# A hybrid conformer and attention layer on one core: first weights in common transfers, two statistics moved, the end reordered

## The chip, the core and the metric

The kernel runs on one core of a Trainium2 chip. The metric is the device time of one execution in microseconds; the number given for a kernel is the median of its runs. The core has TensorE (PE, matrix products into PSUM banks), VectorE (DVE), ScalarE (ACT), GpSimd (POOL) and SyncE (SP), which here only issues transfers (DMA). Each engine works through its own instructions in a fixed order, and waits for the others by semaphores. The order of an engine's instructions is set when the kernel is built; an instruction that waits holds up all that stand behind it on its engine.

## The reference

One layer on x (512 tokens x 2048), float32:

```python
xn = rms_norm(x, attn_norm_g[l])
proj = jnp.einsum("bsd,dc->bsc", xn, w_in[l])
u_val, u_gate, q, k, v = jnp.split(proj, split_pts, axis=-1)
y_conv = conformer_conv(u_val, u_gate, ...)      # GLU, depthwise conv 31, LayerNorm, silu
y_na = neighborhood_attention(heads(q), heads(k), heads(v), rpb[l])
mixed = concat([rms_norm(y_conv, conv_out_g[l]), rms_norm(y_na, na_out_g[l])])
x = x + jnp.einsum("bsc,cd->bsd", mixed, w_out[l])
xn = rms_norm(x, ffn_norm_g[l])
up = depthwise_conv(jnp.einsum("bsd,df->bsf", xn, w_up[l]), ffn_dw_w[l], ffn_dw_b[l])
gate, val = jnp.split(up, 2, axis=-1)
x = x + jnp.einsum("bsf,fd->bsd", silu(gate) * val, w_down[l])
return rms_norm(x, final_norm_g)
```

w_in is 2048 x 5120, w_out 2048 x 2048, w_up 2048 x 11264, w_down 5632 x 2048. In the text below "group A" is the convolution half, the first norm, the second norm and the final norm are the three rms_norm over 2048 columns.

## The kernel before, in words

**Arithmetic.** Each float32 operand of a product is split in two parts of the type fp32r, a high part (copied by ACT) and a low part (the rest, subtracted by DVE). A product is three matmuls: high x high, low x high, high x low (mm3, L124 to L129, so L127 to L129 stand for nearly all products). Weights come in units of 128 x 1024 (512 KB): SP loads them into one of 7 buffers "raw" (NR), ACT makes whi (L116), DVE makes wlo (L117), with four buffers each (NW = 4). `weights()` makes units up to three ahead (AHEAD) of the one that PE is at, along a list `plan`; so the whi of a unit is written into the buffer of the unit four earlier, and ACT's copy waits until PE has read that.

**Layout.** Activations lie as [128 columns, 512 tokens] tiles, 16 of them for 2048 columns. The norms' factors are per token, so they are applied after the products. `rsqrt_steps` (L179 to L212) makes such a factor: matmuls against a column of ones add up the squares over the partitions (L190), DVE and ACT take the inverse root (L192, and root in L172 to L177: Sqrt on ACT, four small DVE steps), DVE writes the result on the diagonals of two tiles dg (high L197, low L201, four instructions), and after `rest` yields two matmuls against a matrix of ones spread it over all partitions (L207); ACT copies it out of the bank (L211). Its bank is "po", one buffer, or "sc" with free=True.

**Order.** Statistics are generators. `tick(m)` (L134) stands behind groups of matmuls and takes the next step of the generator at the head of each of two lists, so the number of yields decides behind which product a step is put. `pin` keeps instructions in the order in which they are written; others are ordered by a scheduler's priorities when the kernel is built.

**The start (L214 to L255).** 16 tiles of x are loaded, and for each xh (ACT, times g1) and xl (DVE) are made. The first two output tiles (the gate's first and the value's first) are worked at once, k by k (`project_first`, L327), so that PE can follow the tiles of x as they arrive. Their weights, 2 x 2 units, come in ten transfers of 128 x 256 or 128 x 512 elements, between the tiles of x (`piece`, `pieces`). g1 comes by a DMA that ACT issues. Until the first data are there PE runs 20 matmuls on a tile "warm" that DVE makes (L233 to L240), whose results nobody reads.

**Group A (L372 to L401).** Runs beside the last projections and the attention: mean (L379), squares, the statistic "rln", normalisation and silu of eight tiles (the result, split, is `ma`), squares, the statistic "ra". The output projection starts with `out_half(ma, read_a)`: 16 output groups of 24 matmuls; `read_a` (L580) multiplies each by ra on DVE (oa, L585). There are three PSUM banks "mm" for these groups, so when ra is late the fourth group waits. The attention's last product ao also goes through the bank "po" (L495, copied by ACT in L507, squared in L510).

**Second norm and the MLP's up-projection.** `stats2` (L644) makes rstd2. The up-projection of a block f is a Strassen-like scheme of seven products (c = 0 to 6) of combined weights (`factors`, L655: c = 1, 4 and 6 need DVE additions into a tile ws, c = 2 into a raw) with combined inputs xc (L596 to L634). `up_apart` (L793) does it for f = 0 to 3 with 24 matmuls of 256 columns a product. For f = 0 the first three products run interleaved (L811). Banks: "mm" (three) for c = 0 to 5, "po" for c = 6 (L798). ACT copies the first two results (vv, L823), DVE adds the third; the fourth is copied in L826. `hidden` (L844) multiplies the two results by rstd2, does the depthwise convolution, silu and the product.

**The end (L910 to L998).** The last four f's part of the down-projection is computed last. For the first 384 tokens (fm) the output is kept transposed: 16 tiles, eight pairs, each multiplied by the final norm's factor (`finish`, L925) on DVE or, for some, by ACT and POOL (L932, L933), and sent out by SP (L937, L939), 3.1 MB in all. The last 128 tokens (tm) are computed token by token in four banks of 512 columns (L971 to L987), whose factor needs the sum of squares over all four banks (L981, L986 to L990); then four transfers of 256 KB (L998). `spread` puts the third statistic's L207 (by `next(stats)`), the copy rb (L966) and one pair at a time between the groups of these last matmuls.

## Time and profile before

| | |
|---|---|
| median of 3 runs | 2033.53 us (2030.55 to 2034.37) |
| profiled execution | 2030.16 us, its span 2028.4 us |
| granted clock, mean | 0.998 |
| ACT busy | 1050.9 us (52%) |
| DVE busy | 1675.5 us (83%) |
| bytes moved | 276.41 MB, 135 GB/s over the span |
| matmuls | 10672 |
| output tail: last matmul starts | 2018.94 us |

In rows of a timeline the first two numbers are the start and the busy time of one instruction, or of a run of equal ones (xN, then the busy time of all); then engine, line, operation, what is written <- what is read, shapes. The bracket at the end is the idle time of that engine just before and what ended it. Matmuls overlap in the records: the pace is read from start to start. "L127 MATMUL pu<-xc,whi" is the matmul of line 127 that writes a tile named pu. A row of windows has: the stretch, its length, busy time and number of instructions of PE, weight load, DVE, ACT and POOL, the granted clock, the share of the DMA engines, GB/s.

### The profile page before, as it was taken

The page shows a single profiled execution, that of the slowest core. Times are in us where ns is not written, and L with a number is a line of the kernel's source. Part 1 is how long each engine was busy: PE and PEld are TensorE (multiplying, and loading weights), DVE is VectorE, ACT ScalarE, POOL GpSimd, SP SyncE. Part 2 cuts the span into 40 slices and gives each one's busy share as a digit, 9 for nine tenths or more (in the row PEclk, how much of TensorE's full clock was granted, in tenths as well). Part 3 has the DMA queues.
Part 4 walks back from the last instruction along what each step waited for, and adds up shares of the span by engine and source line. Part 5 has one row for each costly group of instructions (what it writes and reads, how often), then busy time and mean ns, then how long its engine had stood idle before and what let it go on. Part 6 is the DMA issues. An engine that isn't in the chain of part 4 may idle for free.

```text
span 2028.4 us, 28313 instructions
## 1 busy us (share of the span) xinstructions
PE 2015.4 (99%) x10672; PEld 1726.5 (85%) x10672; DVE 1675.5 (83%) x2298; ACT 1050.9 (52%) x1674; POOL 159.5 (8%) x188
## 2 busy tenths in 40 slices
PE   9999999999999999999999999999999999999998
PEld 7888888888888998888888888888888888888887
DVE  7986888988577898888888888888888888889875
ACT  7323344466346555555555555555555555555563
POOL 0000000000001001111111111111111111110111
PEclk9999999999999999999999999999999999999999
DMA  7232333336347435566565565565565565564583
GB/s 256 83 104 84 114 94 109 109 124 215 108 120 178 120 114 146 123 147 146 125 146 146 128 142 146 128 142 146 121 149 146 125 146 146 127 144 127 144 206 126
DMA packets 97784, 276.41 MB, mean 136 GB/s; under 512 B 10992, under 2 KB 12784, under 8 KB 97648
## 3 DMA queue, kind: packets, MB, share of 16 engines
q1 hardware_dynamic: 72288, 228.45, 36.3%
q0 software_dynamic: 25216, 46.15, 15.5%
q8 instruction: 84, 1.38, 0.3%
q14 instruction: 52, 0.43, 0.1%
q10 hardware_dynamic: 144, 0.01, 0.0%
HBM read 220.04 MB, written 54.53 MB: 135 GB/s over the span
## 4 chain that ended last, share of the span: by engine, by line
PE 96%; DVE 2%; DMA 1%; ACT 0%; issue 0%; SPq 0%; ACTq 0%; DVEq 0%
PE pu L718 25%; PE pu L724 13%; PE pd L129 8%; PE pd L127 8%; PE pd L128 8%; PE pj L127 5%; PE pj L128 5%; PE pj L129 5%; PE po L127 3%; PE po L128 2%; PE po L129 2%; PE pv L313 1%; PE pv L312 1%; PE pv L314 1%; PE pu L127 1%; PE pu L129 1%
## 5 line engine op out<-in xcount | busy, mean ns | idle before, releaser
L116 ACT ACTIVATE whi<-raw 128x1024 fp32r<-128x1024 f32 x364 | 384.4, 1058 | 503.8 <-PE pj L128 136.6
L117 DVE TENSOR_TENSOR wlo<-raw,whi 128x1024 fp32r<-128x1024 f32 x364 | 444.4, 1221 | 214.0 <-ACT whi L116 205.2
L718 PE MATMUL pu<-xc,whi 128*128 128x512 f32 x2240 | 552.9, 391 | 0.0
L718 PEld LDWEIGHTS pu<-xc,whi 128*128 128x128 f32 x2240 | 413.0, 188 | 79.1
L724 PEld LDWEIGHTS pu<-xc,wlo 128*128 128x128 f32 x2240 | 292.3, 191 | 13.9
L724 PE MATMUL pu<-xc,wlo 128*128 128x256 f32 x2240 | 296.6, 283 | 0.0
L129 PE MATMUL pd<-hh,wlo 128*128 128x512 f32 x640 | 250.1, 391 | 0.0
L127 PE MATMUL pd<-hh,whi 128*128 128x512 f32 x640 | 249.6, 390 | 0.0
L128 PE MATMUL pd<-hl,whi 128*128 128x512 f32 x640 | 249.3, 390 | 0.0
L871 POOL DMA_DIRECT2D x2d<-pdc x160 | 139.4, 873 | 1162.4 <-ACT pdc L870 837.4
L128 PE MATMUL pj<-xl,whi 128*128 128x512 f32 x512 | 200.2, 391 | 0.1
L129 PE MATMUL pj<-xh,wlo 128*128 128x512 f32 x512 | 200.0, 391 | 0.0
L127 PE MATMUL pj<-xh,whi 128*128 128x512 f32 x512 | 198.9, 393 | 0.0
L750 ACT ACTIVATE pl<-pu 128x256 f32<-128x256 f32 x280 | 104.6, 382 | 143.5 <-PE pu L718 136.4
L116 ACT ACTIVATE whi<-ws 128x1024 fp32r<-128x1024 f32 x132 | 139.8, 1059 | 75.2 <-PE pu L718 58.2
L366 DVE SCALAR_TENSOR_TENSOR y<-ch,prm,y 128x500 f32<-128x500 f32 (+14 forms) x240 | 173.3, 740 | 4.3
L117 DVE TENSOR_TENSOR wlo<-ws,whi 128x1024 fp32r<-128x1024 f32 x132 | 161.1, 1220 | 13.9 <-ACT whi L116 13.6
L129 PEld LDWEIGHTS pd<-hh,wlo 128*128 128x128 f32 x640 | 120.1, 188 | 28.5 <-DVE wlo L117 3.3
L128 PEld LDWEIGHTS pd<-hl,whi 128*128 128x128 f32 x640 | 120.2, 188 | 24.9 <-DVE hl L856 0.3
L127 PEld LDWEIGHTS pd<-hh,whi 128*128 128x128 f32 x640 | 120.4, 188 | 22.6
L870 ACT ACTIVATE pdc<-pd 128x512 f32<-128x512 f32 x160 | 93.8, 588 | 79.3 <-PE pd L129 65.9
L127 PEld LDWEIGHTS pj<-xh,whi 128*128 128x128 f32 x512 | 96.3, 188 | 20.7 <-ACT xh L249 0.2
(204 smaller groups left out, 2886.4 us busy)
## 6 DMA issues: line engine op xcount, KB each, us to landing
raw<-in_w_up SPq DMA_DIRECT2D x176, 512.0 KB, 3.7
raw<-in_w_down SPq DMA_DIRECT2D x88, 512.0 KB, 4.0
x2d<-pdc POOLq DMA_DIRECT2D x160, 256.0 KB, 4.8
raw<-in_w_in SPq DMA_DIRECT2D x60, 512.0 KB, 3.8
raw<-in_w_out SPq DMA_DIRECT2D x32, 512.0 KB, 3.8
raw<-in_w_v SPq DMA_DIRECT2D x16, 512.0 KB, 4.1
tab<-in_tab SPq DMA_DIRECT2D x32, 256.0 KB, 5.0
x<-in_xG SPq DMA_DIRECT2D x16, 256.0 KB, 5.4
```

Source lines behind the costliest of these rows:

```text
L116: i = nc.scalar.activation(hi[:, :n], raw[:, :n], AF.Copy)
L117: j = nc.vector.tensor_sub(lo[:, :n], raw[:, :n], hi[:, :n].bitcast(F32))
L127: nc.tensor.matmul(ps, hi[:, a], mh, start=start, stop=False)
L128: nc.tensor.matmul(ps, hi[:, a], ml, start=False, stop=False)
L129: return nc.tensor.matmul(ps, lo[:, a], mh, start=False, stop=stop)
L312: nc.tensor.matmul(ps, xh, wh[:, f], start=kk == 0, stop=False)
L366: nc.vector.scalar_tensor_tensor(y[:, a:b], h[:, a + j - PAD:b + j - PAD], prm[:, o + j:o + j + 1], y[:, a:b], op0=ALU.mult, op1=ALU.add)
L718: i = nc.tensor.matmul(ps, w[0][:, k * P:(k + 1) * P], comb[c][k], start=k == 0, stop=stop and k == ks[-1])
L724: i = nc.tensor.matmul(ps[:, H:], w[1][:, k * P:(k + 1) * P], comb[c][k][:, :H], start=False, stop=stop and k == U - 1)
L750: nc.scalar.activation(to, ps, AF.Copy)
L870: nc.scalar.activation(t, ps, AF.Copy)
L871: nc.gpsimd.dma_start(xd[d], t, accum_op=ALU.add)
```

## The change

It has five parts.

1. **Start.** The host puts x0 and the 16 columns of g1 in one array x0 (128 x 528), loaded in one transfer into a "raw" buffer; ACT's DMA for g1 is gone, and g1 is copied to its tile by DVE. The weights of the two first output tiles are interleaved by k in one array w_a (128 x 4096), loaded in five pieces, k = 0; 1 to 3; 4 to 7; 8 to 11; 12 to 15, with rows of 1, 3, 4, 4 and 4 KB, issued behind x0, x1, x2, x6 and x10. For x0 the high part is made by DVE. The tile "warm" is a memset and the first thing on DVE; PE runs 7 idle matmuls.
2. **Group A.** One yield more ahead of "rln", one fewer ahead of "ra".
3. **First f.** Its product c = 3 uses the bank "po", and its c = 6 one of the banks "mm".
4. **Second norm.** rest = 4 instead of 2, so L207 comes two products later; the multiplication of the first f by rstd2 and all behind it (`gated_tile`) is issued in f = 1 behind c = 1 (`meanwhile`).
5. **End.** The four banks alternate between "sc" and "tr"; both L207 and rb come at (g, k) = (2, 2) of `spread` or ahead of it, from where on two pairs are finished per step; the sum over three banks is made ahead of the third bank's product with the gains; -0.5 v is made while ACT takes the root, which leaves one DVE step fewer behind it.

The order of instructions in the changed kernel, where it differs: on ACT, the weight copy whi that stood behind ra's copy (L211) stands ahead of the attention's ao (L507), sq and ra; the root (L173) of the second norm stands behind the copy whi of the next f's third product instead of ahead of it. On DVE, that norm's small steps and its dg come each behind one more unit of weight work, in the order 1/root, wlo, step, ws, step, wlo, step, ws, dg (L197), wlo, dg (L201, four). On PE, ra's two L207 stand directly ahead of the fourth output group instead of five matmuls earlier, and rstd2's two stand together behind the first product of f = 1 instead of inside it. On SP only the start and the end differ; on POOL nothing moves.

```diff
@@ -93 +92 @@
     pin = tc.keep_in_program_order
     g1 = consts.tile([P, KD], F32, name="g1")
-    pin(nc.scalar.dma_start(g1, par[:, POFF["g1"]:POFF["g1"] + KD]))
     prm = consts.tile([P, NPAR], F32, name="prm")
     def pc(name, i):
         o = POFF[name] + i
         return prm[:, o:o + 1]
+    warm = t2("warm", F32R)
+    pin(nc.vector.memset(warm.bitcast(F32), 1.0))
     ones_r = consts.tile([P, P], F32R, name="ones")
     ones = ones_r.bitcast(F32)
     nc.vector.memset(ones, 1.0)
@@ -213 +213 @@
     xs, x1 = [], []
     acc1 = t2("acc1")
-    early = [[], []]
-
-    def piece(u, j, c0, c1):
-
-        if c0 == 0:
-            early[j].append((t4([P, U * P], "raw"), wpool.tile([P, U * P], F32R, tag="whi", name="whi", bufs=NW),
-                             wpool.tile([P, U * P], F32R, tag="wlo", name="wlo", bufs=NW)))
-        n = (NC_, 0)[j]
-        raw, hi, lo = (t[:, c0 * P:c1 * P] for t in early[j][u])
-        pin(nc.sync.dma_start(raw, w_in[n, :, (u * U + c0) * P:(u * U + c1) * P]))
-        pin(nc.scalar.activation(hi, raw, AF.Copy))
-        pin(nc.vector.tensor_sub(lo, raw, hi.bitcast(F32)))
+    early = []
+    xg0 = t4([P, U * P], "raw")[:, :S + KD]
+    pin(nc.sync.dma_start(xg0, x0))
+
+    def piece(k0, k1):
+
+        if k0 % CH == 0:
+            early.append((t4([P, U * P], "raw"), wpool.tile([P, U * P], F32R, tag="whi", name="whi", bufs=NW),
+                          wpool.tile([P, U * P], F32R, tag="wlo", name="wlo", bufs=NW)))
+        o = k0 // CH * U * P
+        pin(nc.sync.dma_start(early[-1][0][:, 2 * k0 * P - o:2 * k1 * P - o], w_a[:, 2 * k0 * P:2 * k1 * P]))
+        for k in range(k0, k1):
+            if k % 2 and k > k0:
+                continue
+            raw, hi, lo = (t[:, 2 * k * P - o:2 * min(k // 2 * 2 + 2, k1) * P - o] for t in early[-1])
+            pin(nc.scalar.activation(hi, raw, AF.Copy))
+            pin(nc.vector.tensor_sub(lo, raw, hi.bitcast(F32)))
     idle = consts.tile([P, 1], F32, name="idle")
     pin(nc.scalar.activation(idle, ones[:, 0:1], AF.Square))
-    warm = t2("warm", F32R)
-    pin(nc.vector.tensor_copy(warm.rearrange("p (i k) -> p i k", k=P), ones.unsqueeze(1).broadcast_to([P, S // P, P])))
     ps = psa.tile([P, 2, S], F32, tag="sc", name="idle")
-    for n in (S, S) + 3 * (H,) + 3 * (H - 32,):
+    for n in 6 * (S,) + (H,):
         pin(nc.tensor.matmul(ps[:, 0, :n], warm[:, :P], warm[:, :n], start=True, stop=True))
-    for n in (S, S) + 4 * (H,):
-        for j in range(2):
-            rows = slice(j * DH, (j + 1) * DH)
-            pin(nc.tensor.matmul(ps[:, j, :n], warm[rows, :P], warm[rows, :n], start=True, stop=True))
-
-
-    pieces = {k: [(u, j, c0, c1) for j in range(2)]
-              for k, u, c0, c1 in ((0, 0, 0, 2), (2, 0, 2, 4), (4, 0, 4, 8), (6, 1, 0, 4), (9, 1, 4, 8))}
+
+    pieces = {0: (0, 1), 1: (1, 4), 2: (4, 8), 6: (8, 12), 10: (12, 16)}
     for k in range(KD):
-        x1.append(t2("x"))
-        last = pin(nc.sync.dma_start(x1[k], xG[k]))
+        if k:
+            x1.append(t2("x"))
+            last = pin(nc.sync.dma_start(x1[k], xG[k - 1]))
+        else:
+            x1.append(xg0[:, :S])
         h, l = t2("xh", F32R), t2("xl", F32R)
-        pin(nc.scalar.activation(h, x1[k], AF.Copy, scale=g1[:, k:k + 1]))
-        pin(nc.vector.scalar_tensor_tensor(l, x1[k], g1[:, k:k + 1], h.bitcast(F32), op0=ALU.mult, op1=ALU.subtract))
+        g = g1[:, k:k + 1] if k else xg0[:, S:S + 1]
+        if k:
+            pin(nc.scalar.activation(h, x1[k], AF.Copy, scale=g))
+        else:
+            pin(nc.vector.tensor_scalar(h, x1[k], g, None, op0=ALU.mult))
+        pin(nc.vector.scalar_tensor_tensor(l, x1[k], g, h.bitcast(F32), op0=ALU.mult, op1=ALU.subtract))
         xs.append((h, l))
-        for c in pieces.get(k, ()):
-            piece(*c)
+        if k in pieces:
+            piece(*pieces[k])
+        if k == 0:
+            pin(nc.vector.tensor_copy(g1, xg0[:, S:]))
     with tc.issue_after(last.ins):
         nc.sync.dma_start(prm, par)
     a_, q_, v_ = iter(range(NC_)), iter(range(NP_)), iter(range(2))
@@ -331 +337 @@
         both = [psa.tile([P, S], F32, tag="tr", name="pj", bufs=2) for _ in range(2)]
         for kk in range(KD):
             for j in range(2):
-                m = mm3(both[j], early[j][kk // U][1:], kk % U, xs[kk][0], xs[kk][1], kk == 0, kk == KD - 1)
+                m = mm3(both[j], early[kk // CH][1:], kk % CH * 2 + j, xs[kk][0], xs[kk][1], kk == 0, kk == KD - 1)
             if kk % 4 == 3:
                 tick(m)
         return both
@@ -385 +391 @@
             sum_sq(acc, ys[i], i == 0)
             if i == NC_ // 2 - 1:
                 yield
-        yield
-        yield
+        for _ in range(3):
+            yield
         r = yield from rsqrt_steps(acc, CONV, "rln")
         acc = t2("acc")
         for i in range(NC_):
@@ -396 +402 @@
             sum_sq(acc, ys[i], i == 0)
             if i % 2:
                 yield
-        for _ in range(RA_AFTER):
-            yield
+        yield
         ra.append((yield from rsqrt_steps(acc, CONV, "ra")))
@@ -793 +798 @@
     def up_apart(f, between):
         def begin(c):
-            return weights(), (psa.tile([P, S], F32, tag="po", name="pu") if c == 6 else
+            return weights(), (psa.tile([P, S], F32, tag="po", name="pu") if c == (6 if f else 3) else
                                psm.tile([P, S], F32, tag="mm", name="pu"))[:, :H]
         def part(c, w, ps, ks):
@@ -842 +847 @@
         return y
     def hidden(f, between):
-        g, v = (up_apart if f < CH else up)(f, between)
+        return gated_tile(f, *(up_apart if f < CH else up)(f, between))
+
+    def gated_tile(f, g, v):
         nc.vector.tensor_mul(g, g, rstd2[0])
         nc.vector.tensor_mul(v, v, rstd2[0])
         g, v = conv3(g, f), conv3(v, NF + f)
@@ -877 +884 @@
             pend[-1] = in_two(pend[-1])
         down(pend, down_units(c, i, at))
+    def meanwhile(c, i, at):
+        if (c, i, at) == (0, 1, 1):
+            hs[0] = gated_tile(0, *hs[0])
+        behind(c, i, at)
+
     for c in range(NCH):
         hs = []
         for i in range(CH):
+            if not c and not i:
+                hs.append(up_apart(0, lambda at: None))
+                continue
             last = c == NCH - 1 and i == CH - 1
             if c and i == CH - 1:
                 hs = [in_two(h) for h in hs]
-            hs.append(hidden(c * CH + i, lambda at: None if last else behind(c, i, at)))
+            hs.append(hidden(c * CH + i, lambda at: None if last else meanwhile(c, i, at)))
         if c != NCH - 2:
             hs = [h if isinstance(h, tuple) else in_two(h) for h in hs]
         if not last:
@@ -947 +962 @@
         sum_sq(acc[:, fm], x2[d][:, fm], d == 0, to=fm)
     wide = psa.tile([P, 2, S], F32, tag="sc", name="pt")
-    banks = [wide[:, 0], wide[:, 1]] + [psa.tile([P, S], F32, tag="tr", name="pt", bufs=2) for _ in range(2)]
+    banks = [psa.tile([P, S], F32, tag="tr", name="pt", bufs=2) if g % 2 else wide[:, g // 2] for g in range(CH)]
     stats, rb, xg = rsqrt_steps(acc, D, "rstd3", to=fm, keep=False), [], []
     sums, v, r, y = (sm.tile([P, CH], F32, tag="rs" + c, name="rs" + c) for c in "lvry")
     v, r, y = (t[:, :1] for t in (v, r, y))
@@ -956 +971 @@
     def spread(g, k):
         if (g, k) == (0, 1):
             next(stats)
-        elif (g, k) == (1, 0):
+        elif (g, k) == (2, 2):
             try:
                 next(stats)
             except StopIteration as e:
                 rb.append(e.value)
-            finish(pairs.pop(0), rb[0], split=True)
             rb.append(t2("rb")[:, fm])
             nc.scalar.activation(rb[1], rb[0], AF.Copy)
-        elif rb and pairs:
-            at = pairs.pop(0)
+        for at in pairs[:2 if rb else 0]:
+            pairs.remove(at)
             finish(at, rb[at % 3 == 1], at % 3 == 1, at % 3 != 1)
     for g, ps in enumerate(banks):
         for i in range(CH):
-            nc.tensor.matmul(ps[:, i * P:(i + 1) * P], x2[g * CH + i][:, tm], ident, start=i == 0, stop=False,
-                             is_transpose=True)
+            m = nc.tensor.matmul(ps[:, i * P:(i + 1) * P], x2[g * CH + i][:, tm], ident, start=i == 0, stop=False,
+                                 is_transpose=True)
+            if g == CH - 1 and i == 0:
+                pin(m)
         for k in range(n):
             (hh, hl), (dh, dl) = hs[k], ws[g * CH + k]
-            nc.tensor.matmul(ps, hh[:, tm], dh, start=False, stop=False)
+            i = nc.tensor.matmul(ps, hh[:, tm], dh, start=False, stop=False)
+            if (g, k) == (2, 3):
+                pin(i)
             nc.tensor.matmul(ps, hl[:, tm], dh, start=False, stop=False)
             nc.tensor.matmul(ps, hh[:, tm], dl, start=False, stop=k == n - 1)
             spread(g, k)
         nc.scalar.activation(t2("sq"), ps, AF.Square, accum_out=sums[:, g:g + 1])
+        if g == CH - 2:
+            nc.vector.tensor_reduce(v, sums[:, :CH - 1], axis=AX.X, op=ALU.add)
+            nc.vector.tensor_scalar(v, v, 1.0 / D, EPS, op0=ALU.mult, op1=ALU.add)
         xg.append(t2("xg"))
         if g < CH - 1:
             nc.vector.tensor_mul(xg[g], ps, gains[g])
-        if g == CH - 2:
-            nc.vector.tensor_reduce(v, sums[:, :CH - 1], axis=AX.X, op=ALU.add)
-            nc.vector.tensor_scalar(v, v, 1.0 / D, EPS, op0=ALU.mult, op1=ALU.add)
     assert not pairs
     nc.vector.scalar_tensor_tensor(v, sums[:, CH - 1:], 1.0 / D, v, op0=ALU.mult, op1=ALU.add)
-    root(r, y, v)
+    nc.scalar.activation(r, v, AF.Sqrt)
+    nc.vector.tensor_scalar(v, v, -0.5, None, op0=ALU.mult)
+    nc.vector.reciprocal(r, r)
+    nc.vector.scalar_tensor_tensor(y, r, v, r, op0=ALU.mult, op1=ALU.mult)
+    nc.vector.scalar_tensor_tensor(y, y, 1.5, r, op0=ALU.add, op1=ALU.mult)
     for g in range(CH):
         if g == CH - 1:
             nc.vector.scalar_tensor_tensor(xg[g], banks[g], y, gains[g], op0=ALU.mult, op1=ALU.mult)
@@ -1016 +1038 @@
     a = {n: np.asarray(v) for n, v in inputs.items()}
     xT = np.ascontiguousarray(a["x"][0].T).reshape(KD, P, S)
     xG = np.ascontiguousarray(xT.reshape(KD, P, WH, NG, 8).transpose(0, 1, 3, 2, 4)).reshape(KD, P, S)
+    x0, xG = np.concatenate([xG[0], _cols(a["attn_norm_g"][0])], axis=1), np.ascontiguousarray(xG[1:])
     wi = a["w_in"][0]
     w_in = np.ascontiguousarray(_units(wi[:, :2 * CONV + 2 * NA]))
+    w_a = np.stack([w_in[n].reshape(P, KD, P) for n in (NC_, 0)], axis=2).reshape(P, -1)
     w_v = np.ascontiguousarray(wi[:, 2 * CONV + 2 * NA:].reshape(KD // 2, 2, P, 2, S).transpose(3, 0, 2, 1, 4)
                                ).reshape(2, KD // 2, P, 2 * S)
     wo = a["w_out"][0]
```

10 lines of the change are left out of this document (4 added, 6 removed).

## The prediction

> **What bounds the kernel now.** I read the page's first lines, then all waits of TensorE (PE) in one table, and only then timelines of the stretches that the change touches.
>
> ```profile
> span 2028.4 us, 28313 instructions
> ...
> PE 2015.4 (99%) x10672; PEld 1726.5 (85%) x10672; DVE 1675.5 (83%) x2298; ACT 1050.9 (52%) x1674; POOL 159.5 (8%) x188
> ```
>
> ```profile
> PE idle L236 <- DVE warm L233: 1.6, 1, 1.6
> PE pu L127 <- ACT vv L823: 1.5, 1, 1.5
> PE st L190 <- DVE acc L170: 0.3, 1, 0.3
> PE po L127 <- DVE oa L585: 0.3, 1, 0.3
> ```
>
> PE is busy for 2015.4 of 2028.4 us. The second table (what PE waited for, total us, times, longest) is all that it waits for once it has begun: 1.5 us at the first f's fourth product, 0.3 at one statistic, 0.3 at the first use of ra. The change removes no matmul but idle ones, so it can gain only in these three places, in the first microseconds and behind the last matmul; it can lose wherever a wait is put into an order in which PE had none. All times below are those of the profile before, as if each part were changed alone.
>
> **Part 1, the start.** The rows of PE, of ACT, and two windows (the last column is GB/s):
>
> ```profile
> 6.05 0.80 PE L127 MATMUL pj<-xh,whi 128*128 128x512 f32 x1
> ...
> 7.85 0.39 PE L128 MATMUL pj<-xl,whi 128*128 128x512 f32 x1
> 8.08 0.40 PE L129 MATMUL pj<-xh,wlo 128*128 128x512 f32 x1
> ...
> 16.50 0.71 PE L127 MATMUL pj<-xh,whi 128*128 128x512 f32 x2
> 17.26 0.50 PE L128 MATMUL pj<-xl,whi 128*128 128x512 f32 x1
> ```
>
> ```profile
> 3.77 0.72 ACT L249 ACTIVATE xh<-x,g 128x512 fp32r<-128x512 f32 x1 [1.09 <-DMA g<-in_par]
> ```
>
> ```profile
> 3.00:5.00 2.00, 2.00 (x10) 1.68 (x10) 0.48 (x1) 1.03 (x2) 0.00 (x0) 1.00 0.64 171
> ...
> 22.00:29.00 7.00, 7.00 (x33) 5.79 (x32) 6.32 (x10) 6.23 (x10) 0.00 (x0) 1.00 1.03 407
> ```
>
> The first real matmul starts at 6.05. The one at 7.85 is followed after 0.23 us, the pace of 512 columns with a warm clock; the four between 6.05 and 7.85 took 1.80 instead of 0.92. Two matmuls from 16.50 to 17.26 take 0.76 instead of 0.46: a stall of 0.3. The change drops the transfer of g1, waits for x0 with its factors at most until 3.77, lets DVE make xh0, and runs 7 idle matmuls instead of 20. Even at ACT's 0.72 for xh0 the first real matmul is possible at 4.5. That alone gains nothing: PE then arrives at the next tiles of x before they do. What counts is how early the data come. From 3 to 5 us the chip moved 171 GB/s and later 407, which loses 2 x (1 - 171/407) = 1.16 us of transfer; ten pieces of weights become five with longer rows. If that hole closes, the start gains 1.16 (bound -1.2). Against it, 512 KB of weights for k = 4 to 7 now stand in SP's queue ahead of x3, and their copies ahead of xh3 on ACT: at 407 GB/s 1.29 us late (bound +1.3). I take **-0.2**, between them and near the row of the 0.3 stall, which goes because those weights then come before they are needed; what is late next is x3.
>
> The Trainium skill ("DMA: Bandwidth & Descriptors", section "Bandwidth") holds that small transfers are descriptor-dominated and that gathering them raises the rate. The hole of 171 GB/s among pieces of 1 and 2 KB rows agrees; by that rule alone the start would gain its whole 1.16.
>
> **Part 2, group A's statistics.** One more yield moves the first statistic (L190 for rln) 24 matmuls later, one fewer brings ra forward.
>
> ```profile
> 431.38 0.39 PE L129 MATMUL pj<-xh,wlo 128*128 128x512 f32 x1
> 432.07 0.72 PE L190 MATMUL st<-ones,acc 128*128 128x1 f32 x5 [0.31 <-DVE acc L170]
> ```
>
> ```profile
> 499.18 0.62 PE L207 MATMUL st<-dg,ones 128*128 128x512 f32 x2
> ...
> 500.57 0.39 PE L129 MATMUL po<-mah,wlo 128*128 128x512 f32 x1
> 501.22 0.50 PE L127 MATMUL po<-mah,whi 128*128 128x512 f32 x1 [0.26 <-DVE oa L585]
> ```
>
> ```profile
> 497.83 0.58 ACT L507 ACTIVATE ao<-po 128x512 f32<-128x512 f32 x1
> ...
> 499.84 0.60 ACT L211 ACTIVATE ra<-st 128x512 f32<-128x512 f32 x1 [0.76 <-PE st L207]
> 500.77 1.06 ACT L116 ACTIVATE whi<-raw 128x1024 fp32r<-128x1024 f32 x1 [0.33 <-PE po L128]
> ```
>
> ```profile
> 500.47 1.29 DVE L585 TENSOR_TENSOR oa<-po,ra 128x512 f32<-128x512 f32 x2 [0.67 <-ACT ra L211]
> ```
>
> From 431.38 to 432.07 are 0.69 us instead of 0.23, so moving L190 gains 0.47. Its chain then runs 24 x 0.23 = 5.5 us later, under products of other tiles; the table of waits has no wait for what it feeds (ma), so I cost that at nothing (without that cover, PE would wait for ma up to those 5.5 us).
>
> For ra the order on ACT matters. Before, ACT does ao, sq, ra and only then the weight copy whi of 500.77, which waits until PE has read the buffer's last weights (here the end of the third output group, 0.20 after the start of its last matmul at 500.57). In the changed kernel this copy stands ahead of ao, so ao, sq and ra are queued behind PE's third group, and PE's L207, which shares the bank of ao, waits for ao. L207 itself stands directly ahead of the fourth group, which needs a bank that only oa frees. Step by step: the third group's last matmul starts at 500.57 - 0.47 - 0.46 (two L207 that now come later) = 499.64; whi 499.84 to 500.85; ao until 501.4; L207 at 501.45; ra 0.66 after it (as 499.18 to 499.84), 502.1; oa 0.63 later, 502.75; PE 0.75 after that (500.47 to 501.22), 503.5. Before it went on at 501.22, so the part costs **+2.3**, the gain of 0.47 within. Bounds: -0.5 if whi finds its buffer free earlier, +2.8 if the 0.47 is not gained either.
>
> **Parts 3 and 4, first f and second norm.**
>
> ```profile
> 678.68 0.28 PE L128 MATMUL pu<-xc,whi 128*128 128x256 f32 x1
> 678.80 0.28 PE L129 MATMUL pu<-xc,wlo 128*128 128x256 f32 x1
> 680.61 0.39 PE L127 MATMUL pu<-xc,whi 128*128 128x256 f32 x1 [1.53 <-ACT vv L823]
> ...
> 686.47 0.95 PE L190 MATMUL st<-ones,acc 128*128 128x1 f32 x8
> ...
> 695.66 0.40 PE L207 MATMUL st<-dg,ones 128*128 128x512 f32 x1
> ...
> 696.73 0.28 PE L127 MATMUL pu<-xc,whi 128*128 128x256 f32 x1
> ```
>
> ```profile
> 680.19 0.64 ACT L823 ACTIVATE vv<-pu 128x256 f32<-128x256 f32 x2
> ...
> 687.66 0.20 ACT L173 ACTIVATE rsr<-rsv 128x4 f32<-128x4 f32 x1
> 690.37 1.06 ACT L116 ACTIVATE whi<-raw 128x1024 fp32r<-128x1024 f32 x1 [2.51 <-PE pu L128]
> ```
>
> ```profile
> 692.61 0.68 DVE L197 TENSOR_TENSOR dg<-ident,rsy 128x512 fp32r<-128x512 f32 x1
> 693.21 1.22 DVE L673 TENSOR_TENSOR ws<-ws,raw 128x1024 f32<-128x1024 f32 x1
> 694.35 1.13 DVE L201 SCALAR_TENSOR_TENSOR dg<-ident,rsy,dg 128x128 fp32r<-128x128 f32 x4
> ```
>
> The fourth product waited for a bank that the vv copies (680.19) free. In the idle bank "po" it starts at 678.80 + 0.12 = 678.92: a gain of 1.69. Then five products of 24 x 0.12 = 2.88 us (c = 3 to 6 and f1's first) and the statistic of 0.95 bring PE to 694.27. Before, the two L207 stood apart inside f1's first product, the second at 695.66; now both stand behind it, at 694.27, and f1's second product, at 696.73 before, could start at 694.27 + 0.46 = 694.73, a gain of 2.0 if the factor is ready.
>
> It is not. Before, the root (L173) ran on ACT at 687.66, ahead of the copy whi of 690.37, which waits for PE. Now it stands behind that copy (f1's third weights, whose buffer is free when c = 5 ends). c = 5 ends at 678.92 + 3 x 2.88 + 0.95 = 688.5; the copy takes until 689.65, the root until 689.8. On DVE the short steps behind it alternate with weight work, in order: wlo, ws, wlo, ws, then dg, wlo, and the four L201. From start to start ws is 1.14 (693.21 to 694.35), wlo is of the same size, dg 0.60, four L201 1.05. The second wlo waits for a copy that follows c = 6 (ends 691.4): 692.6 to 693.75; ws to 694.9; dg to 695.6; the third wlo, whose copy follows f1's first product, to 696.75; L201 to 697.8. PE's second L207 follows at 697.85 and the second product near 698.2: **+1.45** against 696.73. PE waits about 3.5 us there, in two pieces, some 1.4 for dg and 2.0 for L201. Bounds: -2.0 with no wait, +2.6 with one more DVE pass of 1.14 ahead of L201. hs[0] gated later only moves DVE work to where PE has weights ahead; I cost it at nothing, covered by f1's third and fourth products (without it, 1.14 for each full DVE pass that comes ahead of a wlo).
>
> **Part 5, the end.**
>
> ```profile
> 2014.00:2017.50 3.50, 3.50 (x17) 2.84 (x16) 2.98 (x6) 1.43 (x4) 2.98 (x4) 1.00 0.51 183
> 2017.50:2027.00 9.50, 1.83 (x9) 1.17 (x7) 4.75 (x14) 2.50 (x7) 2.90 (x3) 0.71 1.01 374
> ```
>
> ```profile
> 2014.52 5.88 POOL L933 TENSOR_TENSOR fin<-x,rb 128x384 f32<-128x384 f32 x6 [39.61 <-ACT rb L966]
> ```
>
> ```profile
> 2013.94 0.49 ACT L966 ACTIVATE rb<-st 128x384 f32<-128x384 f32 x1 [3.83 <-DVE fin L935]
> ```
>
> ```profile
> 2018.94 0.39 PE L979 MATMUL pt<-dl,hh 128*128 128x512 f32 x1
> ```
>
> The last matmul starts at 2018.94, but the tail is the 4.19 MB of outputs: 0.64 MB leave by 2017.5 (183 x 3.5), the other 3.55 at 374 GB/s until 2027.0. The five root steps behind the last sum are one fewer now, but xg's transfers queue behind this stream, so that gains nothing. What counts is when the stream begins. Copying rb no longer waits for a first pair on DVE, and two pairs are issued per step, so POOL starts some 1 us earlier and its first pair no longer holds up SP's queue. With 374 GB/s from 2014.7 on, 4.19 MB end at 2025.9: -1.1. Pairs that come late leave holes, so I take **-0.6**; bounds -1.2 and +0.3 (the two L207, now side by side, wait as the L190 of 432.07 did).
>
> **The sum.** -0.2 + 2.3 + 1.45 - 0.6 = **+2.95** on the profiled execution (2030.16, span 2028.4), which becomes 2033.1. The median of the runs shown, 2033.53, lies 3.37 above it, so I predict a median of **2036.5**. Bounds of the parts add to -4.9 and +7.0.
>
> **Rivals.**
> - *The waits don't bite.* If weight buffers free up before ACT gets to them, parts 2 to 4 gain -0.47 and -2.0: -0.2 - 0.47 - 2.0 - 0.6 = -3.3, **2030.2**. For it: ACT is busy only 52%. Against it: both copies have a PE releaser in their rows (500.77, 690.37). Chance 0.25.
> - *Slower, by the clock.* PE's new stall at the second norm, 3.5 us, lowers its clock. Before, PE began at 1.6 and was at full pace only from 7.85: 6.2 us at half pace cost 3.1. The point that decides is an idle time above the 1.53 of 680.61, after which the pace was unharmed. 2036.5 + 3.1 = **2039.6**. Against it: the stall is in two pieces, and the granted clock of the windows' rows is 1.00 from 3 to 5 us already, when the pace was still half. Chance 0.10. The Trainium skill ("TensorE: Matmul & The Clock Gate", Part 1) has the clock fall back after an idle window of about 3.4 us; by that rule neither piece is long enough, and the trace so far agrees only up to 1.53.
> - *The start loses.* The hole in the transfers stays and x3 is 1.29 late: +1.5 against my -0.2, **2038.0**. For it: what makes the hole is not visible. Chance 0.12.
>
> **How the numbers follow.** The forecast has 0.53, with its own range 2034.5 to 2038.5. A measurement of this kernel tells about 0.2% (4.07 us) from no change, so "faster" ends at 2029.5 and "slower" begins at 2037.6. Faster: a third of the first rival, 0.08. Slower: the clock 0.10, two thirds of the third rival 0.08, a quarter of the forecast 0.13, together 0.31. Same: 0.61. The range 2030 to 2040 leaves out about half of the first rival (0.12) and of the second (0.05).
>
> **What would show it.** Start: first real matmul near 4.5 and no stall like that of 17.26; a GB/s of 3 to 5 us well above 171 would speak for -1.2. Part 2: no wait for acc near 432, the weight copy ahead of ao on ACT, and two PE waits near 500 of together 3 us. Parts 3 and 4: no wait for vv near 679; waits of PE's L207 for DVE's dg (1.4 and 2.0) near 694 to 698. If those waits are missing, the first rival holds. A pace of 0.24 instead of 0.12 behind 698 would show the second. End: POOL starts 1 us earlier against the last matmul, whose start is 9.5 us from the span's end now and would be about 8.9.

## The result and the profile after

The changed kernel took 2037.71 us (median of 11 runs, 2036.94 to 2039.87); the kernel before, run beside it, 2030.86 (11 runs, 2030.04 to 2034.37). The ratio is 1.0034, 95% interval 1.0026 to 1.0042: slower by about 7 us. The profiled execution took 2037.17, its span is 2035.4 (before: 2030.16 and 2028.4). So on like executions the loss is 7.0 us, where the prediction had 2.95. That its 2036.5 comes close is luck: the three runs it started from had a median 2.7 us above the one that eleven runs gave. (Eight of before's eleven times lie between 2030.04 and 2031.27, three between 2032.82 and 2034.37, and two of those three were among the ones it had.)

The page's line of busy times and PE's waits (total us, times, longest), of the kernel after:

```profile
PE 2016.9 (99%) x10659; PEld 1727.2 (85%) x10659; DVE 1676.3 (82%) x2299; ACT 1050.2 (52%) x1673; POOL 159.7 (8%) x188
```

```profile
PE st L207 <- DVE dg L201: 1.6, 1, 1.6
...
PE po L127 <- DVE oa L590: 1.4, 1, 1.4
PE st L207 <- ACT ao L512: 1.4, 1, 1.4
PE st L207 <- DVE dg L197: 1.4, 1, 1.4
PE pj L127 <- ACT whi L231: 1.2, 1, 1.2
PE pj L127 <- ACT xh L251: 0.2, 1, 0.2
```

The waits for vv (1.5) and for acc (0.3) are gone; in their place stand two pairs: 1.4 + 1.4 at ra and 1.4 + 1.6 at the second norm. PE's busy time has grown by 1.5 us with 13 matmuls fewer. That is the second part of the loss, and the timeline of PE shows it. Group A first, then the second norm:

```profile
500.79 0.73 PE L207 MATMUL st<-dg,ones 128*128 128x512 f32 x2 [1.41 <-ACT ao L512]
502.94 0.50 PE L127 MATMUL po<-mah,whi 128*128 128x512 f32 x1 [1.41 <-DVE oa L590]
...
503.65 0.63 PE L129 MATMUL po<-mah,wlo 128*128 128x512 f32 x1
504.07 0.63 PE L127 MATMUL po<-mah,whi 128*128 128x512 f32 x1
...
506.63 0.44 PE L127 MATMUL po<-mah,whi 128*128 128x512 f32 x1
```

```profile
699.07 0.47 PE L207 MATMUL st<-dg,ones 128*128 128x512 f32 x1 [1.37 <-DVE dg L197]
701.16 0.70 PE L207 MATMUL st<-dg,ones 128*128 128x512 f32 x1 [1.63 <-DVE dg L201]
701.67 0.41 PE L127 MATMUL pu<-xc,whi 128*128 128x256 f32 x1
701.88 0.42 PE L128 MATMUL pu<-xc,whi 128*128 128x256 f32 x1
...
704.65 0.31 PE L129 MATMUL pu<-xc,wlo 128*128 128x256 f32 x1
```

Behind each pair of waits the step from matmul to matmul is 0.42 us instead of 0.23 (512 columns) until 506.63, and 0.21 instead of 0.12 (256 columns) until 704.65, with nothing waited for. The windows of those stretches have the cause in the column behind POOL, the granted clock:

```profile
503.00:506.60 3.60, 3.60 (x9) 2.83 (x10) 2.97 (x5) 0.00 (x0) 0.00 (x0) 0.54 0.28 109
506.60:510.00 3.40, 3.40 (x16) 2.79 (x15) 0.00 (x0) 0.00 (x0) 0.00 (x0) 0.98 0.00 0
...
701.60:704.70 3.10, 3.10 (x16) 3.03 (x15) 3.10 (x5) 1.75 (x3) 0.00 (x0) 0.50 0.01 3
704.70:708.00 3.30, 3.30 (x29) 3.30 (x29) 3.30 (x6) 1.70 (x3) 0.00 (x0) 1.00 0.00 0
```

**Where the 7.0 us are.** Counting the product matmuls of both kernels (there are equally many) and comparing the start of each with its counterpart gives the lead or lag of the changed kernel, in us: -0.2 after 50 matmuls; -1.0 at the last ones ahead of ra (the wait for acc gone, statistics moved); +1.7 at 502.94, behind ra's two waits; +3.3 at 506.6, behind the half clock; +1.55 behind the first f's fourth product (its wait gone: -1.8); +4.9 at 701.67, behind the waits for dg; +6.3 behind the second half clock, and so until the last matmul, which starts at 2025.25. The rest, 0.7, is the tail: from there to the span's end are 10.15 us against 9.46.

### The profile page after: what moved, and what is told of

Its sections match the earlier page's. It is cut to its first block, busy times and chain, and to the rows that moved or that the text cites. A ratio compares the mean times of both kernels' runs of the same rounds, so it can differ in the third digit from the quotient of the medians.

```text
span 2035.4 us, 28280 instructions
## 1 busy us (share of the span) xinstructions
PE 2016.9 (99%) x10659; PEld 1727.2 (85%) x10659; DVE 1676.3 (82%) x2299; ACT 1050.2 (52%) x1673; POOL 159.7 (8%) x188
## 4 chain that ended last, share of the span: by engine, by line
PE 98%; DVE 0%; DMA 0%; ACT 0%; issue 0%; SPq 0%; ACTq 0%
PE pu L723 25%; PE pu L729 13%; PE pd L129 8%; PE pd L127 8%; PE pd L128 8%; PE pj L127 6%; PE pj L128 6%; PE pj L129 6%; PE po L127 3%; PE po L128 3%; PE po L129 3%; PE pv L320 1%; PE pv L318 1%; PE pv L319 1%; PE pu L127 1%; PE pu L128 1%
```

## The experiments

Each ran with the kernel before beside it; medians are of about 11 runs, before's median (28 to 35 runs) was 2030.27 in the first four and 2030.33 in the others. The ratios are those on record and not the quotients of these medians, since before's times lie unevenly here too (beside e5 to e8 21 from 2029.41 to 2030.97 and 14 from 2032.78 to 2035.73). Where the two differ below, both are given.

**e1: the change without part 2** (group A's yields as before).

```diff
-        for _ in range(3):
-            yield
+        yield
+        yield
         r = yield from rsqrt_steps(acc, CONV, "rln")
...
-        yield
+        for _ in range(2):
+            yield
         ra.append((yield from rsqrt_steps(acc, CONV, "ra")))
```

> The changed kernel with the yields of group A as before (part 2 undone). Theory: part 2 costs about 3.4 us of the changed kernel's 6.9 over before: two waits of PE near 500 (3.3 us of idle time, less what moved work regains) and 1.5 us at half clock behind them (granted clock 0.54 from 503.0 to 506.6 in the profile after). So this kernel is 3.4 us faster than the changed one, about 3.4 us above before, without a wait for ao or oa above 0.5 us and with the clock at full pace behind 500. Rival: the two losses aren't additive, since DVE, nearly full in the first f's, bounds the stretch behind; then less than 1 us is gained.

2034.54 us, ratio to before 1.0020 (1.0011 to 1.0029). The median is 4.3 above before's, and in the trace nothing is lost around 500 (the lag is 0.5 at 475 and at 506); no half clock there. Part 2 costs what the lags said, from -0.2 to +3.3.

**e2: before with the bank alone** (part 3, L798).

```diff
-            return weights(), (psa.tile([P, S], F32, tag="po", name="pu") if c == 6 else
+            return weights(), (psa.tile([P, S], F32, tag="po", name="pu") if c == (6 if f else 3) else
```

> The kernel before with the first f's fourth product in bank po and nothing else (part 3 alone; rest stays 2). Theory A: the bank alone makes the order in which the root stands behind the weight copy on ACT and dg behind weight work on DVE; then the 1.6 us gained at the fourth product are paid back with the wait for dg (two pieces, 3.0 us in all) and 1.3 us at half clock: 2.5 to 3.2 us slower than before. Theory B (as the prediction had it): the later factor of part 4 does that; then the bank alone gains its 1.6 us, and PE waits for no dg.

2033.39 us, ratio 1.0014 (1.0005 to 1.0023): theory A. This one line, with rest still 2, gives the order that the prediction had put down to the later factor:

```profile
PE st L207 <- DVE dg L201: 1.6, 1, 1.6
PE st L207 <- DVE dg L197: 1.4, 1, 1.4
```

```profile
697.50:701.00 3.50, 3.50 (x17) 3.44 (x17) 3.50 (x5) 2.04 (x4) 0.00 (x0) 0.50 0.01 2
```

The wait for vv is gone, the two for dg are there, and the clock is at half behind them. On ACT the root starts at 688.90, right behind the weight copy of 687.93, as in the change and not as before. The order is made by a scheduler when the kernel is built; only the bank was altered, and the root stands elsewhere. Why the scheduler places it there was not looked into.

**e3: the change with the wait filled by idle matmuls.**

```diff
+FILL = 12
...
+        for _ in range(FILL if free else 0):
+            nc.tensor.matmul(ps, ones_r, comb[0][0], start=True, stop=True)
         for i, dg in enumerate(ds):
             nc.tensor.matmul(ps, ones_r, dg, start=i == 0, stop=i == 1)
```

> The changed kernel with 12 matmuls of 512 columns, whose results nobody reads, directly ahead of the second norm's two spreading matmuls, into the same bank: PE works for 2.6 us where it waited for dg, and the waits end no sooner. Theory: the half clock behind that place (16 us-long rows of 0.21 instead of 0.12 from 701.67 to 704.65) comes from PE's idle time just before; with idle time cut to some 0.6 us it stays at full pace, 1.3 us faster than the changed kernel. Rival: the slow pace comes from operands or weights that arrive late; then the pace stays 0.21 and the time stays that of the changed kernel, or grows.

2036.17 us (6 runs), ratio 1.0031 (1.0019 to 1.0043); by the times alone not to be told from the change. The trace, of the fastest of the six (2034.56), tells:

```profile
696.42 2.91 PE L208 MATMUL st<-xc,ones 128*128 128x512 f32 x12
699.17 0.39 PE L210 MATMUL st<-dg,ones 128*128 128x512 f32 x1
700.04 0.50 PE L210 MATMUL st<-dg,ones 128*128 128x512 f32 x1 [0.48 <-DVE dg L202]
700.38 0.28 PE L128 MATMUL pu<-xc,whi 128*128 128x256 f32 x1
700.49 0.28 PE L129 MATMUL pu<-xc,whi 128*128 128x256 f32 x1
```

DVE gives dg no sooner, yet the pace behind it is 0.12 at once. Idle time of PE just before causes the slow pace, not the operands. The stretch from the fourth product to behind this place costs 1.4 us here, 2.95 in the change. The same trace holds a second finding, at ra, where nothing was altered:

```profile
501.27 0.73 PE L210 MATMUL st<-dg,ones 128*128 128x512 f32 x2 [1.41 <-ACT ao L515]
503.41 0.50 PE L128 MATMUL po<-mah,whi 128*128 128x512 f32 x1 [1.41 <-DVE oa L593]
503.75 0.40 PE L129 MATMUL po<-mal,whi 128*128 128x512 f32 x1
503.99 0.39 PE L130 MATMUL po<-mah,wlo 128*128 128x512 f32 x1
```

The same two waits to a hundredth, 0.47 us later in the execution, and the pace stays 0.23. The same idle time can lower the clock in one execution and not in another; what tells the two apart is worked out behind the experiments.

**e4: before with the reordered end alone** (part 5; the diff is that of the change from `wide = ` on).

> The kernel before with the reordered end and nothing else (part 5 alone). In the profile after the time from the start of the last matmul to the span's end is 10.15 us against 9.46 before. Theory: part 5 itself costs this, since the stream of output transfers begins 1.2 us later against the last matmul than before and its last transfers take longer: 0.4 to 0.9 us slower than before. Rival (the prediction): the stream is full earlier (from 3.1 us ahead of the last matmul instead of 1.4), 0.6 us faster; then the 0.69 of the profile after has another cause.

2030.00 us, ratio 0.9999 (0.9990 to 1.0008): no difference that the times show; from the last matmul's start (2018.93) to the span's end (2028.1) are 9.17 us against 9.46. The end itself gains 0.3, and the 0.7 lost in the change's tail must come from elsewhere.

**e5: the bank, with the root kept early.** Before, e2's line, and in rsqrt_steps:

```diff
+SOON = 300
...
+        with shifted(-SOON if free else 0):
             nc.vector.tensor_scalar(v, ps, 1.0 / n, EPS, op0=ALU.mult, op1=ALU.add)
             root(r, y, v)
...
```

(and the dg steps down to L202 in the same block; a lower number is placed earlier).

> Before with the first f's fourth product in bank po, and the second norm's root, dg and small steps given a higher priority when the order is made, so that the root stands ahead of the weight copy on ACT and dg behind two weight passes instead of four, as in the kernel before. Theory: the bank costs only by that order; with the root early PE waits for dg less than 0.5 us and keeps its pace, and the 1.5 to 1.8 us of the fourth product remain: 1.2 to 2 us faster than before. Rival: PE comes 1.7 us earlier to a DVE that is full there, so the wait comes back in another place (weights, dg) and the time is that of before within 0.5 us.

2028.03 us, ratio 0.9984 (0.9976 to 0.9993): faster. No wait for dg or vv is left among PE's waits inside the kernel:

```profile
PE pj L128 <- ACT xh L252: 0.6, 1, 0.6
PE st L191 <- DVE acc L171: 0.3, 1, 0.3
PE po L128 <- DVE oa L588: 0.3, 1, 0.3
```

So the bank was right, and its price was the order of the short steps of the factor's chain, of which the 0.20 us root is the first. (The root, the small steps and dg were moved together; the root alone was not tried.) The lead grows by 2.1 us from ahead of the fourth product (lag 0.6) to behind f1's first product (-1.5), as the prediction's -2.0 without wait.

**e6: before with three yields ahead of rln and none ahead of ra.**

> Before with one yield more ahead of rln, as in the change, and none (instead of two) ahead of ra. In the order, ra's two spreading matmuls stand some 80 matmuls ahead of where they stood and its weight copy is behind. Theory: ao and ra are no longer queued behind a copy that waits for PE, the wait for acc (0.47) and that for oa (0.42) go: 0.5 to 0.9 us faster than before. Rival: ra's chain, brought forward, holds PE at the spreading matmuls (dg not made yet); then a wait for dg of 1 us or more appears near 480, and the kernel is slower.

2034.10 us, ratio 1.0015 (1.0006 to 1.0025): slower. The rival had that, but not the cause. The profiled execution is one of the slowest, 2037.70:

```profile
PE po L127 <- DVE oa L585: 3.4, 1, 3.4
PE pu L127 <- ACT vv L823: 2.3, 1, 2.3
```

Of the two waits only the first is of this edit: it takes the lag from -1.0 ahead of ra to +3.3 behind the half clock that follows. The second, for vv, is as long in e8, where group A is as before. ra itself is ready early (ACT copies it at 485.82), so PE does not wait at L207; but the copy whi that waits for PE stands ahead of ao all the same, and the fourth output group still waits:

```profile
485.82 0.60 ACT L211 ACTIVATE ra<-st 128x512 f32<-128x512 f32 x1 [0.55 <-PE st L207]
...
499.30 1.06 ACT L116 ACTIVATE whi<-raw 128x1024 fp32r<-128x1024 f32 x1 [0.98 <-PE po L128]
500.27 0.58 ACT L507 ACTIVATE ao<-po 128x512 f32<-128x512 f32 x1
```

DVE then has wlo (500.39, made from that whi), the sum of ao's squares (501.54) and only behind them oa (502.15), whose ra has long been there. So the late copy holds the group through DVE's order too, and an earlier ra alone does not free it.

**e7: before with the changed start alone** (part 1).

> Before with the changed start and nothing else (part 1 alone). The end of the profile after takes 0.69 us longer than before's, though the reordered end alone takes 0.29 less: the four last transfers of 256 KB land 0.8 us apart instead of 0.68, and the span ends 1.3 us behind the last one instead of 0.95. Theory: that comes with the start (other arrays in memory, one transfer issued by ACT less); then this kernel, with the old end, has it too: from the last matmul's start to the span's end 10.1 us, and 0.2 to 0.8 us slower than before in all. Rival: it needs both start and end; then the tail is 9.46, and the time that of before within 0.5 us, by the start's own gain or loss.

2031.57 us, ratio 1.0000 (0.9992 to 1.0009): by the ratio no difference, by the medians 1.2 us slower. The trace has the theory's tail, 10.31 us (last matmul at 2019.59, span 2029.9) with the old end, and on PE a lag of 0.6 after 50 matmuls; its span is 1.5 us longer than before's, more than was expected. The last outputs take longer, by the table of transfers (issue to landing, median); the first line is before's, the second e7's:

```profile
out_N<-xg SPq DMA_DIRECT2D x4, 256.0 KB, 3.2
```

```profile
out_N<-xg SPq DMA_DIRECT2D x4, 256.0 KB, 3.6
```

**e8: before with the later factor alone** (part 4: rest = 4, the first f gated in the second).

> Before with rest = 4 and the first f multiplied by rstd2 behind the second f's second product, and nothing else (part 4 alone). In its order the root stands ahead of the weight copy and the spreading matmuls stand one product later. Theory: part 4 by itself makes no wait; PE finds dg ready, the 1.53 us wait for vv stays, and the time is that of before within 0.5 us. Rival (the prediction): the factor later brings the wait for dg of 3 us and half clock; 3 us slower than before.

2031.68 us, ratio 0.9999 (0.9990 to 1.0009): no wait for dg. The theory held by the ratio (by the medians it is 1.35 slower); the runs spread from 2029.33 to 2035.28, as before's beside them do, and the profiled one, with the line for vv that e6 has, shows one way in which time is lost:

```profile
681.00:684.00 3.00, 3.00 (x15) 3.00 (x15) 3.00 (x4) 0.01 (x1) 0.00 (x0) 0.50 0.00 0
```

The old wait for vv was 2.3 us long here instead of 1.5, since a weight transfer came later in this execution (DVE waits for it for 1.71 us at L668, 0.78 in the profile before), and half clock followed this one idle time. That before's longer times come in this way fits, but no such execution of before was profiled.

**e9: bank, early root and reordered end on before** (e4 and e5 together).

> Before with the fourth product in bank po and the root early (2.3 us faster than before in its median) and with the reordered end (0.27 faster in its median, 0.29 less from the last matmul to the span's end). Theory: the two lie in different stretches and add: 2.2 to 2.9 us faster than before, granted clock at full pace throughout, tail 9.2 us. Rival: the reordered end changes nothing that the median shows; then it is the 2.3 us of the bank alone, tail 9.45.

2027.77 us, ratio 0.9982 (0.9973 to 0.9991), the fastest of all; tail 9.23 us. Against e5's 2028.03 the end adds too little to be measured.

**e10: the change with both orders mended** (part 2 undone as in e1, root early as in e5).

> The changed kernel with part 2 undone and the second norm's root, dg and small steps at a higher priority; start, bank, later factor and reordered end as in the change. Theory: with both order faults gone, what is left of the change is the start (0 to +0.6 on PE), the slower last transfers (+0.7 in the tail), the bank (-1.6): 0 to 1.2 us faster than before, 6 to 7 us faster than the changed kernel. Rival: other parts of the change cost as well, hidden so far; then it is above before.

2029.14 us, ratio 0.9992 (0.9984 to 1.0001), 1.2 faster by the medians; span 2027.4, 8.0 below the change's. All that is lost in the change but the 0.7 of the tail (10.18 here) and 0.3 at the start is thus in the two orders.

**e11 and e12: what makes the tail slow.** e11 is e7 with one more small transfer by ACT; e12 is e7 with the new arrays declared last.

```diff
+    scrap = consts.tile([P, KD], F32, name="scrap")
+    pin(nc.scalar.dma_start(scrap, par[:, :KD]))
```

```diff
-def layer(ctx, tc, xT, xG, x0, w_a, w_in, w_v, w_out, w_up, w_down, par, tab, g3, out, last_out):
+def layer(ctx, tc, xT, xG, w_in, w_v, w_out, w_up, w_down, par, tab, g3, x0, w_a, out, last_out):
```

> The kernel of e7 (before with the changed start) with one small transfer more: ACT loads 16 columns of the parameters into a tile that nobody reads, as it loaded g1 before. Its tail was 10.31 us, with the last four transfers 0.79, 0.85 and 0.65 us apart. Theory Q (queues): the missing transfer of ACT shifts how the later ones are spread or ended; then the tail is 9.46 here. Theory M (memory): the two new arrays shift where the outputs lie; then the tail stays above 10.

> The kernel of e7 with the new arrays x0 and w_a declared behind all other inputs, and xG and the parameters in their old sizes, so that every older input keeps its place against the first one. Theory M: if the place of the inputs matters, the tail falls to 9.46; if only that of the outputs matters (they still come behind 2 MB more), it stays above 10. Theory Q (queues): it stays above 10, and e11's falls.

2031.45 us (ratio 1.0002, 0.9993 to 1.0011) and 2032.44 (1.0005, 0.9996 to 1.0013). The tails are 10.24 and 9.92 us. Over all traces the tail is 9.9 to 10.4 with the changed start and 9.2 to 9.5 with the old one. The missing ACT transfer is not the cause. In e12 the last four transfers take 3.1 us from issue to landing, as without the new arrays (3.1 to 3.2), where the other six traces with the changed start have 3.5 to 3.6: with the inputs in their old places the slower landing is gone, and about half of what was added to the tail went with it (10.31 to 9.92, against 9.46 before). That the outputs lie elsewhere, behind 2 MB more, fits the rest and wasn't tried alone, nor was the smaller number of transfers at the start. The cause of that rest stays open. At the start e12 is worse than e7: PE waits 2.85 us for the second piece of weights, and the lag after 50 matmuls is 1.3.

**What the traces have on the clock.** In the record of the granted clock of all 14 traces, every stretch at one rate, up to the last one, lasts a whole number of 3.413 us (at half rate 3.41 twice in the change, once in e1 and e8, 6.83 in e2). So the steps lie on a grid, which can be counted on from where a trace first reaches the full clock (4.97 us in the change, 7.17 in e3, 4.40 in e12). Windows on this grid in which the waits fall, of the change (at ra and at the second norm), of e3 (at ra) and, with the row of the wait, of e12 (at the start):

```profile
499.90:503.32 3.42, 1.12 (x4) 0.64 (x5) 2.97 (x4) 2.07 (x4) 0.00 (x0) 1.00 0.88 329
697.88:701.29 3.41, 0.59 (x2) 0.31 (x3) 3.41 (x8) 1.12 (x2) 0.00 (x0) 1.00 0.46 159
```

```profile
498.69:502.10 3.41, 1.91 (x8) 0.93 (x6) 1.81 (x3) 2.24 (x4) 0.00 (x0) 1.00 1.06 394
502.10:505.52 3.42, 2.11 (x9) 1.77 (x10) 3.36 (x6) 0.54 (x1) 0.00 (x0) 1.00 0.63 224
```

```profile
9.03 0.50 PE L127 MATMUL pj<-xh,whi 128*128 128x512 f32 x1 [2.85 <-ACT whi L231]
```

```profile
4.40:7.81 3.41, 1.77 (x7) 0.95 (x6) 1.60 (x4) 0.72 (x1) 0.00 (x0) 1.00 0.98 280
7.81:11.23 3.42, 2.20 (x9) 1.63 (x10) 1.89 (x4) 2.31 (x5) 0.00 (x0) 1.00 1.02 386
```

In the change both waits at ra fall in one window, of which PE is busy for 1.12 us, and the next window runs at half clock. In e3 the grid lies otherwise, each wait falls nearly whole in a window of its own, PE is busy for 1.91 and 2.11 us, and the clock stays. In e12 even 2.85 us in one piece, spread over two windows, leave it up. Over all traces, windows at full clock with 0.59 to 1.70 us of work were followed by half clock (seven windows), those with 1.70 (e7) and with 1.77 or more were not: the border lies near half of the window. This was read from the traces afterwards; no run was made to test it.

## Why the prediction was right in its waits and too small in its sum

Of the 4.05 us that the sum lacks (7.0 against 2.95), 2.9 are half clock, which it had as a rival and not as a term, and 1.3 are the end (0.7 lost instead of 0.6 gained). Group A's waits cost 0.35 less than predicted, those of parts 3 and 4 0.2 more.

- **Start, -0.2.** The first real matmul started at 4.39 (4.5 predicted). In the profile after the lead is 0.2, but this is luck: it differs from execution to execution, also by when the clock reaches its full rate (at 4.97 us in the profile after, at 7.72 in that before). Over the seven kernels with the changed start the lag after 50 matmuls lies between -0.2 and +1.3 (mean +0.4, without e12 +0.3), over the seven with the old one, before among them, between -0.7 and +0.6 (mean -0.25). So the start costs half a us or more on PE. What came late was not x3 but the second piece of weights (the profile after):

```profile
5.88 0.39 PE L129 MATMUL pj<-xh,wlo 128*128 128x512 f32 x1
7.42 0.50 PE L127 MATMUL pj<-xh,whi 128*128 128x512 f32 x1 [1.16 <-ACT whi L231]
```

  The window from 3 to 5 us of the profile after:

```profile
3.00:5.00 2.00, 2.00 (x7) 1.47 (x6) 1.40 (x3) 0.42 (x1) 0.00 (x0) 1.00 0.94 237
```

  The chip moved 237 GB/s here and 206 in e7, where it had been 171: the hole closes by 15 to 28% (of 407 - 171), and the piece of k = 1 to 3 (384 KB, in one transfer) is first copied by ACT at 6.96, after a wait of 0.74 us for it. The 0.7 in the tail, which the start brings with it, was in no term.
- **Group A, +2.3.** The order and the steps were right, as ACT's and DVE's rows of the profile after show:

```profile
499.19 1.06 ACT L116 ACTIVATE whi<-raw 128x1024 fp32r<-128x1024 f32 x1 [1.72 <-PE po L128]
500.16 0.58 ACT L512 ACTIVATE ao<-po 128x512 f32<-128x512 f32 x1
...
501.56 0.60 ACT L211 ACTIVATE ra<-st 128x512 f32<-128x512 f32 x1 [0.16 <-PE st L207]
```

```profile
502.19 1.29 DVE L590 TENSOR_TENSOR oa<-po,ra 128x512 f32<-128x512 f32 x2
```

  The copy waits for PE, ao follows, then L207 (500.79), ra, oa and PE (502.94). From the lag of -0.2 to the +1.7 at that point are 1.9 against 2.3. What the term lacked is what follows: 1.6 us at half clock (+1.7 to +3.3).
- **Parts 3 and 4, +1.45.** The waits came as worked out, 1.4 and 1.6 (1.4 and 2.0 predicted); from +3.3 ahead of the fourth product to +4.9 at f1's second are 1.6 against 1.45. Again half clock adds 1.35. The price was right, but the cause was named wrongly where the step speaks of the two L207 and the later factor: e2 and e8 show that the bank alone does it, and that part 4 alone makes no wait.
- **hs[0] later, at nothing.** Held (e8: no wait of PE that it could have caused).
- **The end, -0.6.** The first rows of finished pairs in the profile after, on POOL and on DVE:

```profile
2020.07 5.89 POOL L948 TENSOR_TENSOR fin<-x,rb 128x384 f32<-128x384 f32 x6 [39.48 <-ACT rb L980]
```

```profile
2020.25 3.23 DVE L950 SCALAR_TENSOR_TENSOR fin<-x,prm,st 128x384 f32<-128x384 f32 x6
```

  POOL starts 5.2 us ahead of the last matmul (2025.25) instead of 4.4, near the 1 us predicted. But DVE begins with the pairs 5.0 us ahead of it, later than before (2012.77, 6.2 us ahead), where SP issued the first pair's transfers from 2013.41 on, ahead of POOL's start; only 0.3 remains (e4). In the change the tail lost 0.7, which comes with the changed start (e7).
- **The rivals.** "The waits don't bite" fell. "The clock", with a chance of 0.10 and a price of 3.1, is what happened, in two places, at 1.6 and 1.35, 2.9 in all. What was argued against it, that the stall is in two pieces, was the error: two pieces of 1.4 us with 0.7 us of work between them, and of 1.4 and 1.6 with 0.5, lowered the clock. The other argument, a granted clock of 1.00 from 3 to 5 us at half the pace, was none: in every trace the record of the clock begins where it first reaches the full rate, and ahead of that the rows show 1.00 whatever the pace. The third rival's loss at the start was real (+0.5 or more), though it came by the weights, not by x3.
- **The Trainium skill on the clock** ("TensorE: Matmul & The Clock Gate", Part 1) says that one idle window of about 3.4 us brings half rate back, and that windows run on freely. The first, read as an unbroken idle time of 3.4 us, speaks against what was seen: 2.3 us in one piece (e8) and 1.4 + 1.4 sufficed. The second agrees: the same waits did it in the change and not in e3, and the two half-clock stretches of the profile after end 704.65 - 506.63 = 198.02 us apart, 58 times 3.41. By the windows above, one that is idle for clearly more than half is enough; that fits all traces, but was not tested.

## What to carry to other kernels

Idle time of PE may have to be priced twice: the wait itself, and 1.3 us or more of half clock behind it. Of the nine waits or pairs of waits with 2.3 us of idle time or more in these traces seven were followed by it. What counted was not the longest single wait, but how much of a window of 3.4 us was left idle, so that a short piece of work between two waits is no relief; where the windows lie differs from execution to execution. Read what stands ahead of the short links of a chain in each engine's order: a copy that waits for PE ahead of a 0.2 us root and the steps behind it cost 3 us. An edit that only frees a bank can move such a link, so compare the orders of all engines even for a one-line change, and put the chain's steps first by priority (by the medians e5 is 2.3 us faster than before, where the bank alone, e2, was 3.1 slower).

## What the runs showed of the hardware that was not expected

- Half clock after 1.37 + 1.63, 1.41 + 1.41 and 2.3 us of idle time, none after 1.53 (before), nor after 1.41 + 1.41 in e3 or 2.85 in e12. It is seen in the granted clock (0.50) and lasted one window of 3.41 us in the change and in e8, two (6.83) in e2.
- With two more input arrays, declared ahead of the weights, the last 256 KB outputs took 3.5 to 3.6 us from issue to landing in all six traces, with the old end (e7) as with the new one, against 3.1 to 3.2 in the seven traces without them, and 3.1 with the arrays declared behind the other inputs (e12, one trace). Why the place should matter is open.
